# Griffin recurrent block on one core: four edits to the stretch from the gates to the output projection

## The chip, the cores and the metric

One core of a Trainium2 chip runs the whole program. The metric is device time in microseconds (us) of one execution, the median of several runs. Engines are named as in the profile: PE (matrix products), PEld (its weight loads), DVE (vector), ACT (activations), POOL (GpSimd), SP (whose queue issues every DMA here).

## The reference, cut to what matters

Two layers work on 512 tokens of 1024 features in float32: layer 0 is sparse attention and a feed-forward, layer 1 the recurrent block and a feed-forward. The change lies in the recurrent block (1408 channels):

```python
gate, u = jnp.split(h @ w_in, 2, axis=-1)
u = conv(u) + conv_b
r = sigmoid(u @ w_a + b_a); i_g = sigmoid(u @ w_x + b_x)     # in blocks of 88 channels
log_a = -8 * softplus(-lam) * r
a = exp(log_a)
b = sqrt(-expm1(2 * log_a)) * (i_g * u)
_, hs = associative_scan(lin_rec, (a, b), axis=1)            # hs[t] = a[t] * hs[t-1] + b[t]
y = hs * gelu(gate)
return y @ w_out
```

## The kernel before, in words

Activations lie with features on the 128 partitions and the 512 tokens along the row, so 1408 channels are 11 tiles of 128x512. Every float32 product is made of three (lines 259 to 261): weights and activations are split into a high part (`hi`, rounded to the type that PE multiplies) and the rest (`lo`), and hi*hi, hi*lo and lo*hi are summed in a PSUM bank. `chunk` (line 230) loads 1024 columns of weights through SP's queue into one of four `wraw` buffers and splits them in two halves; `split` (line 244) writes `whi` on ACT (line 248) and `wlo` on the engine that the second letter of `how` names (line 254): "av" is DVE, "ag" is POOL. There are six `whi` and six `wlo` buffers of 512 columns, so halves of three chunks.

The instructions are written as loops, and a scheduler orders them. It goes by the instructions' place in the program, shifted by the table `PRIORITY` (line 122: a negative number means that many instructions later than written), and by when its own model has the inputs and a free buffer ready. Each engine then executes its list strictly in order and waits on semaphores. `after` (line 494) adds an order between two instructions.

The recurrent block is `rg` (line 968). `project(t)` (line 973) makes one 128x512 tile of `h @ w_in` from a chunk of weights: 24 products, with the tiles of `gate` being t = 0 to 10. `conv` and `gates` work tile by tile; `gates` leaves r (sigmoid), u (times the input gate, on POOL, line 1031) and vv (a tanh). Then come:
- line 1045, eight of the eleven gate projections, one PSUM bank each;
- lines 1048 to 1053, per tile: Exp on ACT (line 1049), the square of it on POOL into a slot of kind T (line 1052), and (square + 1) times vv on DVE (line 1053);
- lines 1055 to 1059, per tile: Sqrt on ACT (line 1056), the product with u on DVE (line 1058), the scan along the tokens on DVE (line 1059);
- lines 1062 to 1071, per tile: the gate projection (made here for tiles 8 to 10), Gelu from its bank into a slot of kind T (line 1065), the gating product on DVE (line 1067), and the split of y, `yh` on ACT and `yl` on DVE (through lines 248 and 254);
- the output projection `project_out` (line 398): for each of eight tiles of features, two chunks of weights and 33 products over the eleven y, then the residual and the next block.

All Exps stand ahead of all Sqrts on ACT, and these ahead of all Gelus. On-chip memory is given out in slots of 128x512 (line 137): 28 of kind B, 9 of kind T. At the end of the gates u and r hold 11 slots of B each and vv 3; yh and yl take 22 later. The eight PSUM banks are shared by all products.

Of the kernel before, what the change touches and what calls it, by code (L numbers as in the profile page):

```python
# [32 lines left out]
RT = RW // 128  # L33
# [6 lines left out]
def rg_order():  # L40
    """The channels of the recurrent block, tile by tile. Blocks of 88 straddle the tiles of 128; in an even
    tile the part of the block that goes on in the next tile is first, the part of the block from the tile
    before starts in the middle."""
    order, edge = [], []
    for j in range(RT):
        ch = list(range(128 * j, 128 * j + 128))
        p, q = -(128 * j) % BW, (128 * j + 128) % BW
        edge.append((p, q))
        if j % 2 == 0:
            left, full, right = ch[:p], ch[p:128 - q], ch[128 - q:]  # L50
            ch = right + full[:64 - q] + left + full[64 - q:]
        order += ch
    return np.array(order), edge
# [5 lines left out]
def gate_sources(j):  # L59
    """What the gates of tile j need: [(tile, rows of it)] for each product."""  # L60
    if j % 2:
        ends = [(j - 1, 0, RG_EDGE[j - 1][1]), (j + 1, 64, RG_EDGE[j + 1][0])]
        (k, r0, n), short = sorted(ends, key=lambda e: -e[2])
        return [[(j, 0, 128)], [(k, r0, -(-n // 32) * 32), short]]
    return [[(k, 0, 128)] for k in (j - 1, j, j + 1) if 0 <= k < RT]
# [17 lines left out]
def step(name):  # L83
    """All instructions of a method are issued earlier than they are written, as PRIORITY says."""
    def wrap(f):
        def run(self, *a, **k):
            with self.pri(name):
                return f(self, *a, **k)
        return run
    return wrap  # L90


class Split:
    """A weight chunk in two parts that add up to it, by ranges of columns."""
# [12 lines left out]
class Build:  # L107
    def __init__(self, ctx, tc, ins, out):
# [11 lines left out]
    hold = None  # L120
    # how many instructions earlier than written the steps are issued (a digit: in that phase only)
# [4 lines left out]
        "q": -9, "qk": -33, "qr": 20, "res": 140, "scale": 60, "turn": -8, "up": -100, "ws2": -20  # L126
# [18 lines left out]
    def pair(self, dt=F32, name=None):  # L145
        """Two slots in one of the wide ones."""
        t = self.slot("K", dt, name, 1024)
        return t[:, :512], t[:, 512:]

# [12 lines left out]
    def setup(self):  # L162
# [29 lines left out]
        # [diagonal | compressed 0 | diagonal], [diagonal | 0 | compressed 1], compressed 2 and 3  # L192
# [30 lines left out]
    def behind(self):  # L223
        """A piece of the modulations that are needed later."""
        if self.todo:
            l, m, n = self.todo.pop(0)
            with self.pri("ada"):
                self.ada(l, m, n, self.behind_on)
# [15 lines left out]
    def split(self, full, hi, lo, how="av"):  # L244
        """The two parts, on the engines that how names (act, vector, gpsimd)."""
        nc = self.nc
        if how[0] == "a":
            nc.scalar.activation(hi, full, AF.Copy)  # L248
        elif how[0] == "v":
            nc.vector.tensor_copy(hi, full)  # L250
        else:
            nc.gpsimd.tensor_scalar(hi, full, 1.0, 1.0, op0=OP.mult, op1=OP.mult)
        e = nc.vector if how[1] == "v" else nc.gpsimd
        e.tensor_tensor(lo, full, hi.bitcast(F32), op=OP.subtract)  # L254

    def mm3(self, out, w, x, first, last, **k):
        """out += w.T @ x for split operands (hi, lo)."""
        mm = partial(self.nc.tensor.matmul, **k)
        a = mm(out, w[0], x[0], start=first, stop=False)  # L259
        mm(out, w[0], x[1], start=False, stop=False)  # L260
        return a, mm(out, w[1], x[0], start=False, stop=last)  # L261

# [1 line left out]
    def ada(self, l, m, n, engine):  # L264
        """Column n of modulation m of layer l, a partition for each feature of the tile."""
# [15 lines left out]
    def sq_add(self, n, engine, cs=ALL, apart=(KT - 1,)):  # L281
        """Sum of squares over the tiles of features, when a tile (or its columns cs) is final; a new sum
        starts at the tiles in apart."""
# [14 lines left out]
    def norm_scale(self, cs=ALL, behind=None):  # L298
        """1/rms of the tokens cs, the same in all partitions."""
# [6 lines left out]
        for i, t in enumerate(parts):  # L306
            for j in range(nt):
                # all columns share a bank: its first product clears it
                nc.tensor.matmul(p[:, j:j + 1], t[:, 128 * j:128 * j + 128], self.ones[:, 0:1],
                                 start=i == j == 0, stop=t is parts[-1] and j == nt - 1,  # L310
                                 skip_group_check=True)
# [21 lines left out]
    def modulate(self, l, which, cs, R=None):  # L333
        """The input of a block for the tokens cs."""
# [9 lines left out]
    def first(self, src, ts):  # L344
        """Products of the first weight tiles, half of the tokens before the other half."""
# [52 lines left out]
    def project_out(self, src, h, gate, then):  # L398
        """Adds the output to the residual; the last tiles go half of the tokens by half, so that the
        block after it, then, starts with the first half while the second is on its way."""  # L400
# [29 lines left out]
    def nsa(self):  # L430
# [6 lines left out]
        with tc.tile_pool(name="nsa", bufs=1) as np_:  # L437
            self.np_ = np_
            # keys: [window blocks 3..0 | compressed | selected blocks 0..3]
# [54 lines left out]
    def after(self, later, earlier):  # L494
        """Schedule an instruction behind another one, without a wait."""
# [17 lines left out]
    def key_norm(self, banks, r):  # L513
        """Keys of all tokens, normed, every group's twice side by side."""
# [37 lines left out]
    def blocks(self, kv, ct, engine):  # L552
        """Windows of 32 tokens, stride 16: [(parity, d), pair, (group, window)], and the positions."""
# [7 lines left out]
        for gt in range(2):  # L561
            src = ct[gt].rearrange("p (c r) -> p r c", r=16)
            for gp in range(2):
                ph = slice(64 * gp, 64 * gp + 64)
                for jp in range(2):
                    for q in range(4):
                        # token 16 c + 2 jj + jp, jj in 4 q .. 4 q + 3
# [10 lines left out]
    def compress(self, kv, flat):  # L578
        """Hidden layer over the windows, [hidden, (group, window)]."""
        nc = self.nc  # L580
        b = self.bank("tr")
        for c in range(4):
            w = self.raw(self.ins["cmp_w1"][kv, c], 1024)
            for j in range(4):
                for m in range(2):
                    # two groups of sums share a bank: its first product clears both
# [5 lines left out]
        # what the positions add stands behind the windows of group 0  # L592
# [40 lines left out]
    def sel(self, half, tags):  # L633
        """Keys (half 0) or values (1) of the selected branch, with 24 gates each."""
# [15 lines left out]
    def queries(self, g, tags):  # L650
        """Queries of a group for all tokens, two tiles of tokens in a bank."""
        qb = [self.bank(t) for t in tags]
        for k in range(KT):
# [3 lines left out]
            for i in range(NT):  # L657
                s = slice(128 * i, 128 * i + 128)
                # two groups of sums share a bank: its first product clears both
# [24 lines left out]
    def query_tiles(self, g, qn):  # L684
        """Queries with features on the partitions, both parts of a head in one tile."""
        nc = self.nc
        for j, t in enumerate([self.query_norm(*b) for b in qn]):
# [3 lines left out]
            for i in range(2):  # L691
                # even heads: [hi; lo], odd heads: [lo; hi]
# [20 lines left out]
    def attention(self):  # L713
        """Softmaxes run ahead of the products with the values."""
# [48 lines left out]
    def combine(self, g, i, o):  # L763
        """Heads 0, 2 to partitions 0..63 and heads 1, 3 to 64..127 of two tiles."""
# [13 lines left out]
    def softmax(self, g, i, brs, behind):  # L778
        """Probabilities of 4 heads and 128 queries times their gates, by branch and head."""
# [13 lines left out]
        # columns of the scores, and of the mask that goes onto columns of the scores  # L793
# [11 lines left out]
        for h in range(HPG):  # L805
            bank = banks[0][0] if brs == ("c",) and h else self.bank("sc")
            b = bank[:, 32 * h:32 * h + 32] if brs == ("c",) else bank[:, :n]
            # the sums of all heads share the bank of the compressed branch alone: its first product clears it
# [54 lines left out]
    def room(self, i, brs):  # L863
        """How many items' products must be done before slots for these probabilities are free."""
# [12 lines left out]
    def weigh(self, g, i, brs, P, o, first, last):  # L877
        """o += values.T @ P.T, [high parts; low parts of the values] over the partitions."""
# [9 lines left out]
        for u, (n, srcs, V) in enumerate(units):  # L888
# [5 lines left out]
            if n == 32:  # L894
                # both parts below each other, as the values are twice
# [13 lines left out]
    def w_out(self, part):  # L909
        """Adds what the heads of groups 0 and 1 (part 0) or group 2 give to the residual."""  # L910
# [15 lines left out]
    def w_out_last(self, cs):  # L926
        """The same for group 3 and the tokens cs."""
# [13 lines left out]
    def rg_prepare(self):  # L941
        """-8 softplus(-lam), with log1p as a series that keeps float32's accuracy."""
# [25 lines left out]
    def rg(self):  # L968
# [4 lines left out]
        def project(t):  # L973
            if t in early:
                return early[t]
            w = self.chunk(src[t], 1024, "ag" if t < RT else "av")
# [24 lines left out]
        def gates(j):  # L1001
# [5 lines left out]
            for src in ks:  # L1007
# [3 lines left out]
                # the ends of the blocks that straddle, from both neighbours, in one tile  # L1011
# [35 lines left out]
        # tables of the same function together; 1 - a^2 = tanh(x) (1 + a^2) for a = exp(-x)  # L1047
        for j in range(RT):
# [3 lines left out]
            nc.gpsimd.tensor_tensor(t, r[j], r[j], op=OP.mult)  # L1052
            nc.vector.scalar_tensor_tensor(vv[j], t, 1.0, vv[j], op0=OP.add, op1=OP.mult)
        end = e
        for j in range(RT):
            e = nc.scalar.activation(vv[j], vv[j], AF.Sqrt)
            self.after(e.ins, end.ins.name)
            nc.vector.tensor_tensor(vv[j], vv[j], u[j], op=OP.mult)
            nc.vector.tensor_tensor_scan(vv[j], r[j], vv[j], 0.0, op0=OP.mult, op1=OP.add)
        end = e  # L1060
        y = []
        for j in range(RT):
            b = gb[j] if j < 8 else project(j)
            g = self.slot("T")
# [30 lines left out]
def tiles(w):  # L1095
    """[K, N] -> [N/128, 128, K]: for 128 columns, rows k*128+p side by side on partition p."""
# [5 lines left out]
def rows(w, per):  # L1102
    """[K, N] -> [K/128/per, 128, per*N]."""
# [5 lines left out]
def cols(v):  # L1109
    """[..., n*128] -> [128, ...*n]."""  # L1110
# [64 lines left out]
```

## Time and profile before

| what | value |
|---|---|
| median of 3 runs | 1405.46 us (1404.2 to 1409.65) |
| profiled execution: span from its first to its last instruction | 1403.4 us |
| PE busy | 1326.5 us, 95% |
| DVE / ACT / POOL busy | 838.7 / 640.3 / 299.5 us |
| mean granted clock of PE | 0.983 |

Of the profiled execution the span is given; it is 2.1 us below the median and 0.8 us below the lowest of the three runs. A busy share is an average over stages: in each stage another engine can be the one that the others wait for, so what the change touches is read from windows of the trace. A row of the timeline gives the start, the duration, the engine, the line, the output and inputs, how many alike follow each other, and in brackets the idle time of the engine ahead of it with what ended it.

### The profile page before, as it was taken

The numbers are of one execution on the slowest core, as the hardware profiler recorded it, in microseconds if no ns is written. First come the engines' busy times: TensorE is split into PE (matmuls) and PEld (weight loads), VectorE is DVE, ScalarE is ACT, GpSimd is POOL, SyncE is SP. The second block draws the span as 40 slices with busy tenths as digits, with TensorE's granted clock in tenths as the row PEclk, the third lists the DMA queues.
The fourth block names the chain that finished last, engine by engine and source line by source line (L and its number), as shares of the span: only waits on it lengthen the run. The fifth ranks groups of instructions, "written<-read, shape, count | busy, mean of one in ns | idle before, by whom it ended". The sixth has DMA issues, their size and how long they took to land.

```text
span 1403.4 us, 18620 instructions
## 1 busy us (share of the span) xinstructions
PE 1326.5 (95%) x6703; PEld 1095.8 (78%) x6703; DVE 838.7 (60%) x1649; ACT 640.3 (46%) x1446; POOL 299.5 (21%) x367
## 2 busy tenths in 40 slices
PE   6989989889989999999999999977999999999998
PEld 4789956657778888888888977756888888888887
DVE  7885888888987656665532786496354333333231
ACT  4473678857655333333222654834354333332221
POOL 3541254666340000000010032953100000000000
PEclk9999999999999999999999999998999999999999
DMA  7657300222234666665632232212313233333330
GB/s 261 223 186 255 110 1 1 91 73 70 84 91 152 209 206 198 192 197 174 203 100 87 64 106 87 90 51 77 111 63 120 90 102 94 96 96 104 109 107 29
DMA packets 50062, 167.08 MB, mean 119 GB/s; under 512 B 5553, under 2 KB 6833, under 8 KB 49970
## 3 DMA queue, kind: packets, MB, share of 16 engines
q1 hardware_dynamic: 49970, 165.90, 37.6%
q8 instruction: 52, 0.85, 0.2%
q14 instruction: 40, 0.33, 0.1%
HBM read 163.78 MB, written 2.10 MB: 118 GB/s over the span
## 4 chain that ended last, share of the span: by engine, by line
PE 79%; DVE 7%; issue 5%; ACT 5%; POOL 2%; DMA 1%; POOLq 0%; ACTq 0%; SPq 0%; DVEq 0%
PE bank_sc L259 8%; PE bank_sc L260 8%; PE bank_sc L261 8%; PE bank_tr L259 8%; PE bank_tr L260 8%; PE bank_tr L261 8%; PE bank_mm L259 4%; PE bank_mm L260 4%; PE bank_mm L261 4%; PE bank_pv L261 3%; PE bank_pv L259 3%; PE bank_pv L260 3%; PE bank_tr L892 2%; PE bank_sc L811 1%; PE bank_pv L905 1%
## 5 line engine op out<-in xcount | busy, mean ns | idle before, releaser
L248 ACT ACTIVATE whi<-wraw 128x512 fp32r<-128x512 f32 (+4 forms) x422 | 247.9, 595 | 511.5 <-PE bank_tr L260 178.0
L254 DVE TENSOR_TENSOR wlo<-wraw,whi 128x512 fp32r<-128x512 f32 (+2 forms) x368 | 243.5, 667 | 284.4 <-ACT whi L248 283.3
L271 DVE SCALAR_TENSOR_TENSOR wraw<-wraw,cond 128x1024 f32<-128x1024 f32 x96 | 125.6, 1309 | 73.7 <-DMA wraw<-in_ada_w 72.9
L259 PE MATMUL bank_tr<-hh,whi 128*128 128x512 f32 (+1 forms) x400 | 149.8, 375 | 16.4 <-ACT whi L248 10.5
L261 PE MATMUL bank_tr<-hh,wlo 128*128 128x512 f32 (+1 forms) x400 | 149.1, 373 | 6.5 <-POOL wlo L254 6.5
L260 PE MATMUL bank_tr<-hh,whi 128*128 128x512 f32 (+1 forms) x400 | 149.7, 374 | 0.2
L261 PE MATMUL bank_sc<-hh,wlo 128*128 128x512 f32 (+1 forms) x344 | 131.5, 382 | 1.1 <-POOL wlo L254 1.1
L259 PE MATMUL bank_sc<-hh,whi 128*128 128x512 f32 (+1 forms) x344 | 131.5, 382 | 0.0
L260 PE MATMUL bank_sc<-hh,whi 128*128 128x512 f32 (+1 forms) x344 | 131.2, 381 | 0.0
L295 POOL TENSOR_TENSOR sq<-sq 128x256 f32<-128x256 f32 (+1 forms) x25 | 25.7, 1027 | 391.4 <-ACT sq L286 390.8
L254 POOL TENSOR_TENSOR wlo<-wraw,whi 128x512 fp32r<-128x512 f32 (+1 forms) x66 | 94.4, 1446 | 52.7 <-ACT whi L248 47.6
L259 PEld LDWEIGHTS bank_tr<-hh,whi 128*128 128x128 f32 x400 | 76.7, 192 | 31.8 <-ACT whi L248 10.9
L261 PEld LDWEIGHTS bank_tr<-hh,wlo 128*128 128x128 f32 x400 | 76.8, 192 | 20.0 <-POOL wlo L254 7.3
L260 PEld LDWEIGHTS bank_tr<-hh,whi 128*128 128x128 f32 x400 | 77.1, 193 | 13.5 <-DVE hh L254 0.7
L841 POOL TENSOR_SCALAR p<-p,rr 128x128 f32<-128x128 f32 (+3 forms) x128 | 71.5, 577 | 56.5 <-DVE nm L857 27.3
L857 DVE TENSOR_REDUCE nm<-bank_sc 128x1 f32<-128x32 f32 (+4 forms) x192 | 69.7, 382 | 12.6 <-PE bank_sc L816 10.7
L261 PEld LDWEIGHTS bank_sc<-hh,wlo 128*128 128x128 f32 x344 | 65.5, 190 | 13.8 <-POOL wlo L254 1.8
L860 ACT ACTIVATE p<-bank_sc,nm 128x384 f32<-128x384 f32 (+3 forms) x128 | 66.9, 527 | 18.4 <-DVE nm L857 17.7
L260 PEld LDWEIGHTS bank_sc<-hh,whi 128*128 128x128 f32 x344 | 65.6, 191 | 12.2
L259 PEld LDWEIGHTS bank_sc<-hh,whi 128*128 128x128 f32 x344 | 65.5, 190 | 12.2 <-ACT whi L248 0.2
L248 ACT ACTIVATE ph<-bank_tr 128x512 fp32r<-128x512 f32 (+1 forms) x96 | 55.6, 593 | 17.9 <-PE bank_tr L892 16.6
L811 PE MATMUL bank_sc<-K,qs 128*128 128x288 f32 (+5 forms) x128 | 50.3, 396 | 12.4 <-ACT p L860 12.2
(366 smaller groups left out, 3149.7 us busy)
## 6 DMA issues: line engine op xcount, KB each, us to landing
wraw<-in_ada_w SPq DMA_DIRECT2D x96, 512.0 KB, 4.1
wraw<-in_ffn_in SPq DMA_DIRECT2D x88, 512.0 KB, 3.6
wraw<-in_ffn_out SPq DMA_DIRECT2D x32, 512.0 KB, 3.5
wraw<-in_rg_in SPq DMA_DIRECT2D x22, 512.0 KB, 3.2
wraw<-in_ffn_out SPq DMA_DIRECT2D x16, 384.0 KB, 3.2
x<-in_x SPq DMA_DIRECT2D x16, 256.0 KB, 3.5
wraw<-in_nsa_w SPq DMA_DIRECT2D x8, 512.0 KB, 4.3
wraw<-in_cmp_w SPq DMA_DIRECT2D x8, 512.0 KB, 4.4
```

The costliest lines, as they stand in the source:

```text
L248: nc.scalar.activation(hi, full, AF.Copy)
L254: e.tensor_tensor(lo, full, hi.bitcast(F32), op=OP.subtract)
L259: a = mm(out, w[0], x[0], start=first, stop=False)
L260: mm(out, w[0], x[1], start=False, stop=False)
L261: return a, mm(out, w[1], x[0], start=False, stop=last)
L271: done = engine.scalar_tensor_tensor(w, w, 1.0, self.cond, op0=OP.mult, op1=OP.mult, accum_out=mod)
L295: engine.tensor_tensor(s, s, t, op=OP.add)
L811: m = mm(b, q[:, h], kh[:, ks], start=h == 0 or not one, stop=False, skip_group_check=one)
L841: nc.gpsimd.tensor_scalar(P[br, h], P[br, h], r[:, h, x:x + 1], 1.0, op0=OP.mult, op1=OP.mult)
L857: nc.vector.tensor_reduce(nm[:, h, x:x + 1], b[:, cols[br]] if len(brs) > 1 else b, axis=AX, op=OP.max, negate=True)
L860: nc.scalar.activation(dst, b[:, cols[br]] if len(brs) > 1 else b, AF.Exp, bias=nm[:, h, x:x + 1], accum_out=sm[:, h, x:x + 1])
L892: nc.tensor.transpose(t[:n, 128 * h:128 * h + 128], srcs[h], self.ident)
```

## The change

Four edits in `rg`, and one entry in the priority table (edits to comments and blank lines are left out):

```diff
     PRIORITY = {
...
-        "q": -9, "qk": -33, "qr": 20, "res": 140, "scale": 60, "turn": -8, "up": -100, "ws2": -20
+        "q": -9, "qk": -33, "qr": 20, "res": 140, "scale": 60, "scan": -300, "turn": -8, "up": -100, "ws2": -20
     }
...
         def project(t):
             if t in early:
                 return early[t]
-            w = self.chunk(src[t], 1024, "ag" if t < RT else "av")
+            w = self.chunk(src[t], 1024)
...
             t = self.slot("T")
-            nc.gpsimd.tensor_tensor(t, r[j], r[j], op=OP.mult)
+            nc.scalar.activation(t, r[j], AF.Square)
             nc.vector.scalar_tensor_tensor(vv[j], t, 1.0, vv[j], op0=OP.add, op1=OP.mult)
...
             e = nc.scalar.activation(vv[j], vv[j], AF.Sqrt)
             self.after(e.ins, end.ins.name)
-            nc.vector.tensor_tensor(vv[j], vv[j], u[j], op=OP.mult)
-            nc.vector.tensor_tensor_scan(vv[j], r[j], vv[j], 0.0, op0=OP.mult, op1=OP.add)
+            with self.pri("scan"):
+                nc.vector.tensor_tensor(vv[j], vv[j], u[j], op=OP.mult)
+                nc.vector.tensor_tensor_scan(vv[j], r[j], vv[j], 0.0, op0=OP.mult, op1=OP.add)
...
             b = gb[j] if j < 8 else project(j)
-            g = self.slot("T")
+            g = self.slot("B", name="g")
             e = nc.scalar.activation(g, b, AF.Gelu_apprx_tanh)
```

The `wlo` halves of the eleven gate chunks go from POOL to DVE (22 instructions), the eleven squares from POOL to ACT, the eleven Gelu results from kind T to kind B, and the eleven products with u and the scans are ranked 300 instructions later than written. No other line of the program changes, and no DMA is added or taken away.

## Rows read from the trace of the kernel before

**Rows 1.** The page: busy time of each engine over the span.

```profile
PE 1326.5 (95%) x6703; PEld 1095.8 (78%) x6703; DVE 838.7 (60%) x1649; ACT 640.3 (46%) x1446; POOL 299.5 (21%) x367
```

**Rows 2.** Windows: bounds, length, busy us PE, PEld, DVE, ACT, POOL, clock, DMA.

```profile
870.00:893.70 23.70, 20.39 (x84) 14.68 (x83) 9.50 (x10) 11.55 (x21) 16.09 (x16) 1.00 0.24 77
893.70:937.30 43.60, 43.60 (x193) 35.74 (x191) 32.69 (x24) 28.57 (x47) 36.72 (x26) 1.00 0.25 84
937.30:967.80 30.50, 13.51 (x49) 10.47 (x49) 27.08 (x35) 12.07 (x23) 12.77 (x4) 0.72 0.15 48
967.80:1027.00 59.20, 59.20 (x314) 51.09 (x314) 21.36 (x41) 20.12 (x39) 7.18 (x7) 1.00 0.33 97
```

**Rows 3.** What PE waited for from 840 to 1020: us, times, longest.

```profile
PE bank_tr L259 <- ACT whi L248: 10.5, 1, 10.5
PE bank_tr L261 <- POOL wlo L254: 6.5, 1, 6.5
PE bank_sc L259 <- ACT us L248: 1.2, 1, 1.2
PE bank_sc L261 <- POOL wlo L254: 1.1, 1, 1.1
```

**Rows 4.** PE's timeline, 937 to 968 us.

```profile
937.08 0.39 PE L261 MATMUL bank_sc<-hh,wlo 128*128 128x512 f32 x1
947.92 0.79 PE L259 MATMUL bank_tr<-hh,whi 128*128 128x512 f32 x1 [10.45 <-ACT whi L248]
...
955.68 0.80 PE L261 MATMUL bank_tr<-hh,wlo 128*128 128x512 f32 x1 [6.54 <-POOL wlo L254]
...
957.12 0.63 PE L261 MATMUL bank_tr<-hh,wlo 128*128 128x512 f32 x1
...
967.84 0.39 PE L259 MATMUL bank_mm<-yh,whi 128*128 128x512 f32 x1
```

**Rows 5.** ACT's timeline, 907 to 951 us.

```profile
907.09 1.28 ACT L1056 ACT_TABLE_LOAD   x1
...
927.73 0.63 ACT L1065 ACTIVATE slotT<-bank_tr 128x512 f32<-128x512 f32 x1
946.71 0.63 ACT L248 ACTIVATE yh<-slotT 128x512 fp32r<-128x512 f32 x1 [18.35 <-DVE slotT L1067]
947.25 0.61 ACT L248 ACTIVATE whi<-wraw 128x512 fp32r<-128x512 f32 x1
...
949.85 0.57 ACT L1065 ACTIVATE slotT<-bank_sc 128x512 f32<-128x512 f32 x1
```

**Rows 6.** DVE's timeline, 869 to 949 us.

```profile
869.86 0.74 DVE L994 SCALAR_TENSOR_TENSOR u<-slotT,vec,u 128x509 f32<-128x509 f32 x1
...
921.71 1.78 DVE L1058 TENSOR_TENSOR vv<-vv,u 128x512 f32<-128x512 f32 x1
...
932.28 1.26 DVE L1058 TENSOR_TENSOR vv<-vv,u 128x512 f32<-128x512 f32 x2
...
935.72 1.26 DVE L1058 TENSOR_TENSOR vv<-vv,u 128x512 f32<-128x512 f32 x2
...
946.02 1.86 DVE L1067 TENSOR_TENSOR slotT<-slotT,vv 128x512 f32<-128x512 f32 x3
```

**Rows 7.** One line at a time: ns min/median/max, first and last start (L254: 860 to 975).

```profile
L1053 DVE SCALAR_TENSOR_TENSOR vv<-slotT,vv x11: 1511/1526/1786, 901.8 to 920.0; 128x512 f32<-128x512 f32 x11
L254 POOL TENSOR_TENSOR wlo<-wraw,whi x22: 1282/1724/7682, 879.2 to 959.0; 128x512 fp32r<-128x512 f32 x22
L254 DVE TENSOR_TENSOR wlo<-wraw,whi x16: 285/558/1780, 859.7 to 973.7; 128x512 fp32r<-128x512 f32 x6, 128x256 fp32r<-128x256 f32 x6, 128x384 fp32r<-128x384 f32 x2, 128x128 fp32r<-128x128 f32 x2
L254 DVE TENSOR_TENSOR yl<-slotT,yh x11: 678/681/1002, 947.8 to 970.5; 128x512 fp32r<-128x512 f32 x11
```

**Rows 8.** ACT's timeline, 380 to 412 us: Exp, then Square.

```profile
381.91 0.23 ACT L860 ACTIVATION_READ_ACCUMULATOR p<-bank_sc,nm 128x1 f32 x1
...
390.70 0.42 ACT L286 ACTIVATE sq<-x 128x256 f32<-128x256 f32 x1 [1.26 <-DVE x L368]
```

## The prediction

> **What bounds the kernel now.** I read the page first, then windows over the recurrent block, then what PE waited for, then the timelines of PE, ACT and DVE around the longest wait. PE is busy 95% of the span [rows 1], so only PE's idle or slow time can be won, and only where the change acts. The windows show where that is. In 893.7:937.3 PE is busy without a gap; in 937.3:967.8 it is busy 13.51 of 30.50 us, at a granted clock of 0.72; in 967.8:1027 it is full again, 59.20 of 59.20 us, with DMA busy for a third of the time [rows 2]. So what follows would not absorb a gain: an earlier start of the output projection is an earlier end.
>
> The hole is two waits, 10.5 us for a `whi` from ACT and 6.5 us for a `wlo` from POOL [rows 3]. PE starts its last product before them at 937.08, the next gate projection at 947.92, stops again until 955.68, and reaches the first product of the output projection at 967.84 [rows 4]. After the idle time its products take 0.63 us instead of 0.39 for a while [rows 4]: the lower of the clock's two levels, 1.2 GHz instead of 2.4.
>
> Why ACT is late: after its sixth Gelu at 927.73 it stands for 18.35 us at the first `yh`, which needs the first gating product from DVE; the `whi` that PE wants is the next in ACT's list [rows 5]. Why DVE is late: it has gone through all line-1053 operations (the last at 920.0) and all eleven pairs of product and scan before the first gating product at 946.02 [rows 6, 7]. And these run slowly: line 1053 takes a median of 1526 ns beside POOL's squares and splits [rows 7], against 0.74 us for the same operation in the convolution; two pairs take 3.44 us (932.28 to 935.72) once POOL is quiet, while the first product alone took 1.78 us beside POOL [rows 6]. POOL suffers as well: its `wlo` takes 1282 ns at best and 7682 at worst, the one that PE stands for until 955.68 [rows 4, 7]. So the stage hangs on DVE and POOL slowing each other, and on one instruction in the wrong place of ACT's list.
>
> **The change, part by part.**
>
> *Splits to DVE.* 22 halves leave POOL and cost DVE 0.68 us each, the median of `yl`, the same operation on the same shape [rows 7]; back to back I count 0.61, the step of three gating products in 1.86 us [rows 6]. PE's 6.5 us wait for POOL has no cause left. The halves made before 897 share DVE with the last convolution tile, whose chain PE also waits for (1.2 us), while 1.1 us of waiting for a POOL `wlo` goes [rows 3]. Bounds for that stage: three splits in the convolution's way at the slowest DVE split of the trace, 1.78 us [rows 7], 5.3 us lost; or all of PE's 3.3 us of idle time (23.70 - 20.39) gained [rows 2]. I take 1.0 gained, near the wait that is named, since the convolution waits for other engines too and leaves DVE room (busy 9.50 of 23.70 us [rows 2]).
>
> A DVE split beside POOL work has taken up to 1.78 us where 0.68 is usual [rows 7]. The Trainium skill, "SBUF — State Buffer", section "SBUF: two separate sides", says that a DVE operation with two SBUF inputs and a GpSimd one exclude each other for the whole of the instruction. By that rule each of the three splits would wait out one POOL operation, 3 x (0.68 + 1.28) = 5.9 us lost instead of 1.0 gained, and the sum below would be 12.2 instead of 19.1. The slow rows agree with it; how often the two meet before 897 no row tells.
>
> *Squares to ACT.* The Exps and a few splits end at 907.09 [rows 5]. A Square of half the length takes 0.42 us [rows 8], a copy of the full length 0.63 [rows 5]: eleven add 4.6 to 6.9 us, I take 6.4, near the full length. The Sqrt table (1.28 us [rows 5]) is loaded at about 913.5 and the first Sqrt done at about 915.5. Before, the first product with u started at 921.71, behind line 1053 [rows 6]; at 0.74 us each line 1053 takes DVE 8 us and keeps up with the squares. So ACT's added work is paid by the time that its Sqrts no longer wait for DVE.
>
> *Gelu results in B.* The sixth Gelu runs at 927.73, the seventh at 949.85 [rows 5]: T has nine slots and they are given back late. B has three free when the Gelus begin, and each finished pair gives back two (u and r). With pairs from 915.5 seven are done by 927.7, 17 slots for eight Gelus. Cost nothing, hidden by PE's projections; if the pairs were late, ACT would wait at a Gelu instead.
>
> *Scans ranked later.* Nothing is removed. Wherever a split, a gating product or a `yl` is ready it goes ahead of the next pair, so the first y come out before the last scans, and ACT's first `yh` waits for one or two pairs at most. No DMA moves and SP's list keeps its order; POOL's loses 33 instructions and nothing is put behind a wait there.
>
> *The sum on PE.* After 937.30 two projections of 24 products at 0.226 us (43.60 us for 193 [rows 2]) are left: 10.9 us, so the output projection could start at 948.2, not 967.84 [rows 4]. That is 19.6 us: 17.0 of waits and 2.6 of slow clock and restart.
>
> *Can y keep up?* This is the next limit. DVE from 915.5: eleven pairs at 1.72 = 18.9; gating and `yl`, 22 x 0.61 = 13.4; the eight halves of gate tiles 7 to 10, 4.9; four pieces of the first output weights, 1.9. Together 39.1, so y10 is ready at 954.6 if DVE never idles. PE wants y10 at 948.2 plus 30 products = 955.0. It is a tie. Bounds: no loss, or, if DVE starts the pairs only at 921.71 as before, 921.71 + 39.1 - 955.0 = 5.8 us and a slow restart like the old one, 7 in all. I take 1.5 lost, near the lower end, as the cause of the old start, POOL's squares, is gone.
>
> Total: 19.6 + 1.0 - 1.5 = 19.1 us less. The profiled span would go from 1403.4 to 1384.3. It stands 2.1 us below the median of the runs, which I leave as it is: 1405.46 - 19.1 = **1386.4 us**. Bounds of the terms: 19.6 + 3.3 = 22.9 at best (1382.6), 19.6 - 5.3 - 7 = 7.3 at worst (1398.2).
>
> **The rivals.**
>
> *DVE becomes the bound* (chance 0.20, part of "faster"): the pairs start late or DVE idles between gating and `yl`, and PE stops in the first output tile. With 5.8 to 7 us lost there the gain is 13 to 15 us, about 1392. For it: the tie, and DVE's 27.08 of 30.50 us in the old hole [rows 2]. Against: what fills that window is work that POOL had pushed back.
>
> *Scans behind splits that wait for PE* (chance 0.07 for no change, 0.04 for slower). A `wlo` of the output weights may only overwrite a buffer that PE has finished with. If the new rank puts such splits ahead of the scans in DVE's list, the scans wait for PE and PE then for y. With six buffers, the last piece for the first output tile waits for the end of the projection before the last, 942.8; then 18.9 + 13.4 us bring y10 to 975.1, where the old kernel wanted it at 967.84 + 6.8 = 974.6: no change, 1406. Behind the splits for the second output tile, which wait until 948.2, y10 comes at 980.5, 6 us after the old time: with a slow restart about 1413. It decides from the point where the first scan stands behind the last piece for the first output tile. Against it: the scheduler issues what is ready, and while such a split waits a scan is ready.
>
> *A table load at each switch between Exp and Square* (chance 0.01, slower). If Square were not in the table set that Exp needs, up to 22 loads of 1.28 us [rows 5] would put 28 us on ACT ahead of the Sqrts: pairs from 943.5, y10 at 982.6, 8 us after the old time, about 1414. The rows speak against it: at 390.70 a Square follows the Exp whose sum is read at 381.91, and no load stands between [rows 8]. The Trainium skill, "ScalarE: Activation LUTs", section "Table sets: the hidden batching unit", asks for calls batched by set and names copy, relu, identity and abs as members of every set, not Square; this trace shows the pair without a load.
>
> *The hole stays* (chance 0.04, no change): ACT's list again has a `yh` ahead of the `whi` that PE needs, with DVE far behind. For the full 17 us DVE's first gating product would have to be near 946 again; with pairs from 915.5 and three splits even all eleven pairs first end by 936.3, and PE would lose nothing much. For the old time some further delay of 10 us on DVE is needed, and no row shows one without POOL.
>
> **How the numbers follow.** Half a per cent, 7.0 us, is about what a measurement of this kernel can tell from no change. My forecast's own case has 0.64, with 1382 to 1390; with DVE as the bound (0.20) faster has 0.84. No change has 0.07 + 0.04 = 0.11, slower 0.04 + 0.01 = 0.05. The range from 1381 to 1398 takes in both faster cases and the worst sum of the terms; what lies above it is most of the last 0.16.
>
> **What would show it.** Right: PE without the two waits and at a clock of 1.00 from 893 to 975; the first product on `yh` near 948; POOL idle from 897 on; line 1053 near 0.74 us; gating products between pairs on DVE; no ACT_TABLE_LOAD at the squares' line. Wrong: PE waiting for a `yh` or `yl` in the first output tile for over 6 us; ACT idle for over 10 us at a Gelu or a `yh`; DVE idle while a pair's inputs are ready; a `wlo` on DVE over 1.5 us between 870 and 897 with PE waiting for the convolution; or a change of PE's waits outside 870 to 975, where I expect none.

## The result, and the profile after

The changed kernel takes 1385.61 us, the median of five runs (1384.67 to 1394.47), against 1405.46 before: a ratio of 0.9869, with a 95% interval of 0.984 to 0.9899. Measured once more beside another set of runs of before (median 1407.67), it was 1385.66 us and 0.9836 (0.9806 to 0.9867). The prediction was 1386.4, in a range of 1381 to 1398.

The profiled execution is the longest of the five: 1392.5 us between its first and last instruction. Almost 11 us of that were lost long before the changed code, in the attention part: the edge product, the first product on the gates' last edge tile of 48 rows, starts at 888.09 us instead of 877.17, though every engine's list is the same up to that time. So the two traces are compared from that product on, and the windows below are those of [rows 2], moved by 10.92 us. First the page's busy line of after [rows 1], then the windows (bounds, length, busy us of PE, PEld, DVE, ACT, POOL, clock, DMA).

```profile
PE 1329.4 (95%) x6703; PEld 1097.6 (79%) x6703; DVE 830.6 (60%) x1671; ACT 644.6 (46%) x1457; POOL 245.2 (18%) x334
```

```profile
880.92:904.62 23.70, 21.39 (x89) 15.77 (x88) 10.93 (x15) 12.17 (x23) 10.10 (x11) 1.00 0.26 89
904.62:948.22 43.60, 43.60 (x194) 36.11 (x193) 35.39 (x52) 37.03 (x65) 1.29 (x1) 1.00 0.28 90
948.22:978.72 30.50, 29.39 (x126) 23.26 (x125) 23.30 (x39) 15.04 (x30) 1.29 (x1) 1.00 0.28 83
978.72:1037.92 59.20, 57.47 (x356) 50.97 (x355) 28.35 (x64) 25.97 (x57) 8.53 (x8) 1.00 0.31 97
```

The third row is the old hole: PE is busy 29.39 us of 30.50 where it was 13.51, at a clock of 1.00 where it was 0.72, and POOL does 1.29 us where it did 12.77. PE's 1.7 idle us in the last row lie at the start of the next block, which before came behind the end of the row. Of what PE still waits for in the stretch, three lines, against [rows 3]:

```profile
PE bank_sc L261 <- DVE wlo L254: 1.6, 1, 1.6
...
PE bank_mm L259 <- ACT yh L248: 0.5, 1, 0.5
...
PE bank_mm L260 <- DVE yl L254: 0.5, 2, 0.2
```

Both long waits are gone. The 1.6 us are a gate half on DVE, in the early stage; the other two stand in the first output tile. PE's timeline shows the places, and the landmarks used from here on: the edge product, the first product on `yh`, and the first product of the second output tile (`bank_sc<-yh`), which comes when all eleven y have been used once (in one run, u_scan, after ten; see there).

```profile
888.09 0.49 PE L259 MATMUL bank_tr<-edge,whi 48*128 48x512 f32 x1 [0.46 <-POOL edge L1016]
...
896.84 0.50 PE L261 MATMUL bank_sc<-hh,wlo 128*128 128x512 f32 x1 [1.60 <-DVE wlo L254]
...
957.77 0.39 PE L259 MATMUL bank_mm<-yh,whi 128*128 128x512 f32 x1
...
966.18 0.50 PE L259 MATMUL bank_mm<-yh,whi 128*128 128x512 f32 x1 [0.53 <-ACT yh L248]
966.90 0.50 PE L260 MATMUL bank_mm<-yl,whi 128*128 128x512 f32 x1 [0.22 <-DVE yl L254]
...
967.47 0.39 PE L259 MATMUL bank_sc<-yh,whi 128*128 128x512 f32 x1
```

From the edge product, the first `yh` product comes after 957.77 - 888.09 = 69.68 us; before it was 967.84 - 877.17 = 90.67 [rows 4]. The second tile comes after 79.38 us; before, it was 975.32 - 877.17 = 98.15. The two rows of before:

```profile
877.17 0.49 PE L259 MATMUL bank_tr<-edge,whi 48*128 48x512 f32 x1 [0.46 <-POOL edge L1016]
...
975.32 0.39 PE L259 MATMUL bank_sc<-yh,whi 128*128 128x512 f32 x1
```

I call this last length **the stage**. It is 18.8 us shorter.

Why, on DVE, by its timeline (compare [rows 6]):

```profile
910.51 0.69 DVE L1053 SCALAR_TENSOR_TENSOR vv<-slotT,vv 128x512 f32<-128x512 f32 x1
...
926.32 0.69 DVE L1059 TENSOR_TENSOR vv<-vv,u 128x512 f32<-128x512 f32 x1 [1.09 <-ACT vv L1056]
...
936.72 0.68 DVE L1068 TENSOR_TENSOR g<-g,vv 128x512 f32<-128x512 f32 x1
937.32 1.28 DVE L254 TENSOR_TENSOR wlo<-wraw,whi 128x512 fp32r<-128x512 f32 x2
...
961.41 0.67 DVE L254 TENSOR_TENSOR wlo<-wraw,whi 128x512 fp32r<-128x512 f32 x1
...
963.39 0.68 DVE L254 TENSOR_TENSOR wlo<-wraw,whi 128x512 fp32r<-128x512 f32 x1
...
966.16 0.69 DVE L254 TENSOR_TENSOR yl<-g,yh 128x512 fp32r<-128x512 f32 x1 [0.70 <-ACT yh L248]
```

Line 1053 takes 0.69 us where its median was 1.53 [rows 7]. The first product with u comes 38.23 us after the edge product instead of 44.54, and the first gating product after seven products and five scans, not after all eleven pairs. Directly behind it stand two halves of a gate tile's weights. Between 926.32 and the 0.70 us ahead of the last `yl` the timeline marks no idle time of DVE.

And on ACT: the squares (line 1052), the load for the Sqrts, and the Gelus (compare [rows 5]).

```profile
923.21 1.13 ACT L1052 ACTIVATE slotT<-r 128x512 f32<-128x512 f32 x2
924.36 1.28 ACT L1056 ACT_TABLE_LOAD   x1
925.65 0.63 ACT L1056 ACTIVATE vv<-vv 128x512 f32<-128x512 f32 x1
...
937.43 0.63 ACT L248 ACTIVATE yh<-g 128x512 fp32r<-128x512 f32 x1 [2.48 <-DVE g L1068]
937.97 0.61 ACT L248 ACTIVATE whi<-wraw 128x512 fp32r<-128x512 f32 x1
938.49 0.58 ACT L1066 ACTIVATE g<-bank_tr 128x512 f32<-128x512 f32 x1
```

No load stands between Exp and Square. The first `yh` costs ACT 2.48 us of waiting, not 18.35. And the Gelus no longer run ahead six at a time: from the second on, each comes between two `yh`.

### The profile page after: what moved, and what is told of

The parts are those of the page before. It is cut to its first block, busy times and chain, and to the rows that moved or that the text cites. A ratio compares the mean times of both kernels' runs of the same rounds, so it can differ in the third digit from the quotient of the medians.

```text
span 1392.5 us, 18615 instructions
## 1 busy us (share of the span) xinstructions
PE 1329.4 (95%) x6703; PEld 1097.6 (79%) x6703; DVE 830.6 (60%) x1671; ACT 644.6 (46%) x1457; POOL 245.2 (18%) x334
## 4 chain that ended last, share of the span: by engine, by line
PE 78%; DVE 10%; issue 5%; ACT 5%; DMA 2%; POOL 1%; POOLq 0%; ACTq 0%; SPq 0%; DVEq 0%
PE bank_sc L259 8%; PE bank_sc L260 8%; PE bank_sc L261 8%; PE bank_tr L260 8%; PE bank_tr L259 8%; PE bank_tr L261 8%; PE bank_mm L260 3%; PE bank_mm L259 3%; PE bank_mm L261 3%; PE bank_pv L261 3%; PE bank_pv L259 3%; PE bank_pv L260 3%; PE bank_tr L892 2%; DVE wraw L271 2%; PE bank_sc L811 2%
## 5 line engine op out<-in xcount | busy, mean ns | idle before, releaser
L254 DVE TENSOR_TENSOR wlo<-wraw,whi 128x512 fp32r<-128x512 f32 (+3 forms) x390 | 256.0, 663 | 282.7 <-ACT whi L248 277.4
L841 POOL TENSOR_SCALAR p<-p,rr 128x128 f32<-128x128 f32 (+3 forms) x128 | 71.6, 580 | 56.3 <-DVE rr L832 19.3
L857 DVE TENSOR_REDUCE nm<-bank_sc 128x1 f32<-128x32 f32 (+4 forms) x192 | 69.7, 381 | 16.8 <-PE bank_sc L816 14.2
L860 ACT ACTIVATE p<-bank_sc,nm 128x384 f32<-128x384 f32 (+3 forms) x128 | 66.9, 527 | 18.8 <-DVE nm L857 17.9
L260 PEld LDWEIGHTS bank_sc<-hh,whi 128*128 128x128 f32 x344 | 64.7, 188 | 12.2
L254 POOL TENSOR_TENSOR wlo<-wraw,whi 128x512 fp32r<-128x512 f32 (+1 forms) x44 | 53.5, 1231 | 31.8 <-ACT whi L248 30.8
```

Source lines behind the costliest of these rows:

```text
L841: nc.gpsimd.tensor_scalar(P[br, h], P[br, h], r[:, h, x:x + 1], 1.0, op0=OP.mult, op1=OP.mult)
L857: nc.vector.tensor_reduce(nm[:, h, x:x + 1], b[:, cols[br]] if len(brs) > 1 else b, axis=AX, op=OP.max, negate=True)
L860: nc.scalar.activation(dst, b[:, cols[br]] if len(brs) > 1 else b, AF.Exp, bias=nm[:, h, x:x + 1], accum_out=sm[:, h, x:x + 1])
```

## The experiments

The kernels are compared by the stage, since the whole time varies by some 10 us between executions of one kernel, mostly in the attention part. "First u" is the first product with u on DVE, "first y" the first product on `yh`, both in us after the edge product; "rest" is what is left from the end of the stage to the last instruction. These four come from one profiled execution each. Every ratio is to runs of before beside it on the same chip, whose medians were 1405.46 to 1407.67. The lines of later kernels are shifted by a few.

| kernel | first u | first y | stage | rest | median us (ratio to before, 95%) |
|---|---|---|---|---|---|
| before | 44.5 | 90.7 | 98.15 | 428.0 | 1405.46 |
| after | 38.2 | 69.7 | 79.38 | 425.0 | 1385.61 (0.984 to 0.9899) |
| after_again | 38.3 | 69.7 | 79.46 | 425.0 | 1385.66 (0.9806 to 0.9867) |
| u_split | 39.1 | 71.2 | 86.86 | 428.8 | 1393.64 (0.9901 to 0.9944) |
| u_square | 39.7 | 71.6 | 83.03 | 427.5 | 1393.75 (0.9886 to 0.995) |
| u_scan | 38.2 | 77.7 | 84.53 | 426.3 | 1392.97 (0.987 to 0.9933) |
| u_slot | 38.3 | 74.6 | 82.04 | 425.1 | 1390.46 (0.9862 to 0.9918) |
| o_pool | 38.2 | 84.1 | 91.58 | 427.9 | 1400.73 (0.9933 to 0.9972) |
| u_pool | 44.5 | 85.9 | 94.92 | 427.8 | 1402.65 (0.9946 to 0.9982) |
| v_half | 35.1 | 69.7 | 77.87 | 425.0 | 1384.56 (0.9814 to 0.9872) |
| v_half_again | 35.2 | 69.7 | 77.91 | 427.8 | 1383.25 (0.9799 to 0.9866) |
| v_sqd | 37.5 | 69.7 | 78.94 | 425.1 | 1383.31 (0.9803 to 0.988) |
| v_g2 | 38.2 | 69.7 | 79.03 | 427.5 | 1386.36 (0.9813 to 0.9892) |
| v_halfg2 | 35.1 | 69.7 | 77.17 | 428.3 | 1382.11 (0.9792 to 0.9857) |

**How far to trust the stage.** The changed kernel once more.

> The kernel after once more, unchanged: how far does the length of the stage vary between profiled executions? If it is set by the instructions' own times, 79.2 to 79.6 us again (79.38 in the first profile), whatever the span. If it varies like the span does, by several us, none of the differences below 3 us between the kernels is worth anything.

79.46 against 79.38, with spans of 1385.4 and 1392.5. The second kernel run twice, v_half, gave 77.87 and 77.91. So, as far as two kernels profiled twice can show, differences of a few tenths of a us can be read from the stage, which the medians can't give.

**One edit undone at a time.** u_split gives the low halves of the gate weights back to POOL.

```diff
-            w = self.chunk(src[t], 1024)
+            w = self.chunk(src[t], 1024, "ag" if t < RT else "av")
```

> The change with one edit undone: the low halves of the gate weights back on POOL. 'Stage' is the time from the first product on the 48-row edge tile to the first product of the second output tile; it is 98.2 us in the profile before and 79.4 after, 18.8 of the 21.8 us between the two profiles from that point to the end. Theory A (DVE and POOL slow each other, and a POOL half can take 7.7 us beside a busy DVE): from the first pair on DVE is never idle, so POOL's halves for tiles 8 to 10 take 1.8 to 3.2 us each as before, and PE waits for one of them again; stage 82 to 90 us. Theory B (only the place of instructions in the lists counts; who makes the halves does not): DVE has 13 us less to do, y comes sooner, stage 77 to 79 us.

The stage is 86.86, 7.5 us longer, in the range of theory A (POOL and DVE slow each other); a stage under 79.38 would have said that DVE is better off without the halves, and it did not come. But the path is not the one that A expected: in the last projections PE waits for no half from POOL. It stops at the y, as its waits (first line), a product and two windows show:

```profile
PE bank_mm L259 <- ACT yh L248: 2.3, 4, 0.9
```

```profile
957.86 0.63 PE L261 MATMUL bank_mm<-yh,wlo 128*128 128x512 f32 x1
```

```profile
955.00:960.00 5.00, 3.72 (x8) 1.55 (x8) 4.41 (x9) 3.71 (x8) 0.00 (x0) 0.78 0.14 39
960.00:965.00 5.00, 4.36 (x11) 2.66 (x11) 3.85 (x8) 2.92 (x6) 0.00 (x0) 0.53 0.47 144
```

DVE's scans, products and splits beside POOL take 1.8 to 2.2 us where they take 0.7 to 1.2 alone (the scan of line 1060 has a mean of 1395 ns against 1207 in after). One such scan, and the POOL instruction beside it:

```profile
916.08 2.21 DVE L1060 TENSOR_TENSOR_SCAN vv<-r,vv 128x512 f32<-128x512 f32 x1
```

```profile
915.92 1.29 POOL L254 TENSOR_TENSOR wlo<-wraw,whi 128x512 fp32r<-128x512 f32 x1 [1.70 <-ACT whi L248]
```

So the y come late one by one, PE waits a little at the last ones, and after these waits the clock falls to 0.53 in the second window, near the lower level: the last seven products of the tile take 0.63 to 0.80 us.

u_square gives the squares back to POOL.

```diff
-            nc.scalar.activation(t, r[j], AF.Square)
+            nc.gpsimd.tensor_tensor(t, r[j], r[j], op=OP.mult)
```

> The change with one edit undone: the squares back on POOL. Theory A: eleven squares alone keep POOL busy for 14 to 16 us, line 1053 takes about 1.5 us again beside them, but squares on ACT end at about the same time (the last at 924.3 us in the profile after), so the first pair starts within 2 us of where it does now; stage 78 to 82 us, no difference that the timing can tell. Rival: any work of POOL beside DVE costs PE time; line 1053 would end 5 us or more later and the stage be 84 us or more.

83.03: 3.7 us longer, between what A and the rival gave. Line 1053 has a mean of 1293 ns against 684, so the slowing is there. But the first product with u is only 1.5 us later, since ACT, freed of 6.3 us of squares (eleven of 616 ns), reaches its Sqrts earlier. PE then stops for 1.4 us at a low half from DVE and 1.7 us at a `yh`. That edit moved work as much as it removed a collision.

u_scan takes the rank of product and scan away, u_slot puts the Gelu results back into kind T.

```diff
-        "q": -9, "qk": -33, "qr": 20, "res": 140, "scale": 60, "scan": -300, "turn": -8, "up": -100, "ws2": -20
+        "q": -9, "qk": -33, "qr": 20, "res": 140, "scale": 60, "turn": -8, "up": -100, "ws2": -20
```

> The change with one edit undone: product and scan ranked where they are written. In DVE's list all eleven pairs then stand ahead of the two halves for the gate projection of tile 8. Theory C (the place of the gate halves in DVE's list decides): the pairs start where they do now and end 19.5 us later, the second of these halves is ready about 21 us after the first product, 6 us after PE wants it; PE waits 5 to 7 us for a low half from DVE, and loses 1 to 2 more at the lower clock: stage 85 to 88 us. Theory A alone (POOL was the whole cause): the order on DVE is of no weight, stage 79 to 81 us.

```diff
-            g = self.slot("B", name="g")
+            g = self.slot("T")
```

> The change with one edit undone: the Gelu results back in slots of kind T. The lists then have three Gelus ahead of the first yh, four yh ahead of the next two high halves on ACT, and on DVE five gating products and five yl ahead of the halves for tile 8. Theory C: PE waits about 4 us for the halves of tile 8, and the last y comes 2 to 3 us later than in the change: stage 82 to 85 us. Theory A alone, or the reading of the prediction (the kind of slot costs nothing): stage 79 to 80 us.

u_scan: 84.53, 5.2 us longer; u_slot: 82.04, 2.7 longer. u_slot is in the range of C (the place of instructions in the lists decides), u_scan just short of it. But u_scan's landmark flatters it: there PE starts the second tile ahead of the last y of the first.

```profile
963.86 0.39 PE L259 MATMUL bank_sc<-yh,whi 128*128 128x512 f32 x1
964.53 0.50 PE L259 MATMUL bank_mm<-yh,whi 128*128 128x512 f32 x1 [0.28 <-ACT yh L248]
...
965.59 0.39 PE L261 MATMUL bank_mm<-yh,wlo 128*128 128x512 f32 x1
965.82 0.40 PE L259 MATMUL bank_sc<-yh,whi 128*128 128x512 f32 x1
```

At 965.82 the first tile is done, and three products of the second with it, so like for like the stage is 965.82 - 3 x 0.227 - 879.32 = 85.8 us: 6.4 longer than in after, and within C's range. In u_scan POOL is silent and the first product with u as early as in after. DVE then does all eleven pairs without a pause, and the `wlo` that PE needs comes after them and a gating product; DVE's list, then PE's stop:

```profile
934.83 2.33 DVE L1060 TENSOR_TENSOR_SCAN vv<-r,vv 128x512 f32<-128x512 f32 x2
937.08 0.67 DVE L1068 TENSOR_TENSOR g<-g,vv 128x512 f32<-128x512 f32 x1
937.66 1.29 DVE L254 TENSOR_TENSOR wlo<-wraw,whi 128x512 fp32r<-128x512 f32 x2
```

```profile
938.40 0.80 PE L261 MATMUL bank_sc<-hh,wlo 128*128 128x512 f32 x1 [5.09 <-DVE wlo L254]
```

In u_slot several Gelus run ahead, their `yh` follow, and the gate halves come behind those: PE waits 0.5 us and 0.8 us for a `whi` and 1.0 for a `wlo` (2.3 together, where C had about 4), and its first `yh` product is 4.9 us later than in after. All eleven y are then ready in time (82.04 - 74.56 = 7.48 us for the tile, as before), so 2.2 of the 4.9 come back.

**Two edits together.** o_pool is the kernel before with the work taken off POOL alone, by the diff below; u_pool is its mirror image, after with the same lines put back.

```diff
-            w = self.chunk(src[t], 1024, "ag" if t < RT else "av")
+            w = self.chunk(src[t], 1024)
...
-            nc.gpsimd.tensor_tensor(t, r[j], r[j], op=OP.mult)
+            nc.scalar.activation(t, r[j], AF.Square)
```

> The kernel before with the gate weights' low halves on DVE and the squares on ScalarE, and neither the scan's rank nor the Gelu results in B. The stage is the time from the 48-row edge product to the first product of the second output tile: 98.15 us before, 79.38 after. Theory A (DVE and POOL slow each other, and their work beside each other is most of the 18.8 us): L1053 near 0.69 us, the first product with u about 38 us after the edge product, and 84 to 89 us for the stage, the rest being one stop of PE at a low half that stands behind seven gating products and their yl in DVE's list. Theory C (the order of the lists is most of it): 93 us or more, with PE again waiting over 10 us near the last gate projections. Median by A 1393 to 1397, by C 1401 or more.

> The kernel after with both kinds of POOL work given back (low halves of the gate weights and squares on POOL), the scan's rank and the Gelu results in B kept: the mirror image of the run above. Alone, the two edits cost the stage 7.5 and 3.7 us. Theory A: they add up or more, since the one's POOL time delays the other's: 89 to 95 us, L1053 on DVE 1.3 us or more in the mean, the slow DVE operations at about 1.5 to 1.8 us. Theory C: the order alone holds most of the gain: 85 us or less. Median by A 1397 to 1402, by C 1393 or less.

o_pool: 91.58, which neither theory gave; nor is the median, 1400.73, in the range of either. Relieving POOL alone is worth 98.15 - 91.58 = 6.6 us. Line 1053 is fast (685 ns) and the first product with u as early as in after, as A has it, but PE stops for 12.0 us at one low half:

```profile
950.04 0.80 PE L261 MATMUL bank_sc<-hh,wlo 128*128 128x512 f32 x1 [12.01 <-DVE wlo L254]
```

On DVE that half stands behind eleven pairs, eight gating products and six `yl`, the last of them at 948.70. It is the old hole with DVE in POOL's place.

u_pool: 94.92, at the upper end of A's range; the median, 1402.65, is just above it. Placing alone is worth 98.15 - 94.92 = 3.2 us. Here it is the old hole with the old culprit, the `yh` ahead of the `whi` in ACT's list; first ACT, then PE, then line 1053:

```profile
937.84 0.63 ACT L248 ACTIVATE yh<-g 128x512 fp32r<-128x512 f32 x1 [14.59 <-DVE g L1068]
938.38 0.58 ACT L1066 ACTIVATE g<-bank_tr 128x512 f32<-128x512 f32 x1
938.85 0.62 ACT L248 ACTIVATE whi<-wraw 128x512 fp32r<-128x512 f32 x1
```

```profile
939.52 0.80 PE L259 MATMUL bank_sc<-hh,whi 128*128 128x512 f32 x1 [6.95 <-ACT whi L248]
```

```profile
L1053 DVE SCALAR_TENSOR_TENSOR vv<-slotT,vv 128x512 f32<-128x512 f32 x11 | 17.2, 1614 | 15.4 <-POOL slotT L1052 15.4
```

So of 18.8 us, 6.6 come from POOL's relief alone, 3.2 from the placing alone, and the other 9.0 only from both: a fast DVE that does its work in the wrong order still leaves PE waiting, and a good order on a slow DVE does too. That the four single edits, undone, sum to 7.5 + 3.7 + 6.4 + 2.7 = 20.3, near the 18.8, is chance; by pairs the same sum is 15.5 + 12.2 = 27.7.

**What the last 2.2 us hang on.** In after the first output tile takes 79.38 - 69.69 = 9.7 us instead of 7.48. v_half gives every second square to DVE, which is partly idle while ACT does Exps and squares.

```diff
-            nc.scalar.activation(t, r[j], AF.Square)
+            if j % 2:
+                nc.vector.tensor_tensor(t, r[j], r[j], op=OP.mult)
+            else:
+                nc.scalar.activation(t, r[j], AF.Square)
```

> The kernel after with every second square moved from ScalarE to DVE, where DVE waits for ScalarE anyway. Theory D (from the first Sqrt on DVE is never idle, and PE's 2.2 us of waiting for y in the first output tile are set by the time of that first Sqrt): the Sqrt comes 2.5 to 3.5 us earlier (first product with u 35 to 36 us after the edge product instead of 38.2), the wait for yh and yl goes, and the stage takes 77.0 to 78.0 us instead of 79.38. Rival E (the two halves of the second output tile that stand ahead of the ninth and tenth yl on DVE set it, or y follows PE's projections): the stage stays at 79.0 to 79.8. Median by D 1383 to 1385, by E as after.

> The kernel with every second square on DVE once more, beside the kernel after on the same chip. Theory D: stage 77.7 to 78.1 us again (77.87 in its first profile), 1.3 to 1.7 below after; median 0.5 to 2.5 us below after. Rival (chance): stage as after, 79.2 or more.

77.87 and 77.91, as D had it. The first product with u is 3.1 us earlier and DVE waits only 0.33 us ahead of it, and the two halves of the second output tile still stand ahead of a `yl`, now the tenth and the eleventh. 1.5 of the 2.2 us are gone; three of the last four `yl` still wait for their `yh`, for 0.37 to 0.70 us.

v_sqd puts all squares on DVE.

```diff
-            nc.scalar.activation(t, r[j], AF.Square)
+            nc.vector.tensor_tensor(t, r[j], r[j], op=OP.mult)
```

> The kernel after with all squares on DVE and none on ScalarE. Theory D (DVE's work from the first line 1053 on is what y waits for): six more squares of 0.6 us on DVE than with every second one there are 3.7 us, and DVE had only 1.9 us of idle time left, so y comes later again: stage 78.5 to 81. Rival (ScalarE's time up to the Sqrts is what counts, DVE has room): the first Sqrt comes still earlier and the stage goes to 77.2 or less.

78.94: D again. DVE has no marked idle time from 900 us, in the midst of the squares, to the last `yl`, its first product with u is back at 37.5, and PE waits 1.0 us for a `yh`. Of the three ways to share the squares, half on each engine is the best by the stage; the medians on the same chip (1383.25 and 1383.31) don't tell the last two apart.

v_g2 gives the Gelu results two slots of their own, v_halfg2 joins that to v_half.

```diff
-    SLOTS = {"A": 24, "B": 28, "K": 8, "T": 9}
+    SLOTS = {"A": 24, "B": 28, "K": 8, "T": 7, "G": 2}
...
-            g = self.slot("B", name="g")
+            g = self.slot("G", name="g")
```

> The kernel after with the Gelu results in two slots of their own (T 7, B 28), so that two Gelus instead of one run ahead. Theory F (slots of a kind are handed out in the order of the program, so in B a Gelu comes only after the yl of the tile before, and that puts the gate halves ahead of most y on ScalarE and DVE): with two ahead some gate halves come later and y earlier, the stage lies between 79.4 and 82.0 (82.03 with the results in T, where three to six bunch), the first output product comes later than 69.7 us after the edge product, and the output tile waits less for y. Rival (the kind of slot does not matter, the loss of u_slot is chance): first output product within 0.5 of 69.7 and stage within 0.5 of 79.4.

> Every second square on DVE, and the Gelu results in two slots of their own (T 7). If the two small gains in the stage, 1.5 and 0.35 us, come from different places, they add up: 77.3 to 77.7. If the second is chance or hangs on the same wait for y: 77.8 to 78.3. PE's bare work in the stage is 77.1 us (79.38 less 2.2 us of waiting for y), so below 77.1 by neither.

v_g2: 79.03 with the first `yh` product at 69.70, which are the rival's numbers: what theory F gave for the time did not come. In ACT's list the Gelus do run two ahead, so F's account of the order stands, but one more Gelu ahead costs nothing; u_slot, with three ahead of the first `yh`, lost 2.7 us, and no run lies between. v_halfg2: 77.17, a little under the 77.3 to 77.7 that the sum of the two gains would give, so neither stands in the other's way. PE waits for no y in the stage, and its first output tile takes 7.48 us again. By the stage it beats after by 2.2 to 2.3 us; the medians, 1382.11 and 1385.66 us on the same chip, agree but have intervals that overlap.

## Why the prediction was right, point by point

*The sum.* From the edge product to the last product on an edge of 72 rows, with which the early stage ends (891.14 before, 900.81 after), 13.97 us became 12.72: 1.25 gained, where 1.0 was taken. From there to the first `yh` product, 76.70 became 56.96: 19.7 gained, where 19.6 was worked out. The first output tile grew from 7.48 to 9.70: 2.2 lost, where 1.5 was taken. Together 18.8, where 19.1 was predicted. The medians fell by 19.9 us and, beside the second set of runs, by 22.0. That 1386.4 lies within 1 us of both medians of after is in part luck, since the median of before moved by 2.2 us from one set to the next.

*Splits to DVE: right in kind, wrong in place.* In the early stage POOL's wait and ACT's (1.14 and 1.25 us) were replaced by one of 1.6 on DVE, within the bounds. The slowest half on DVE there took 1.09 us, beside POOL's edge copies. The Trainium skill, "SBUF — State Buffer", section "SBUF: two separate sides", lets a two-input DVE operation and a GpSimd one exclude each other; the 5.9 us that this could have cost by the prediction's estimate did not come, while u_pool's line 1053, 1614 ns against 684, agrees with it. That "PE's 6.5 us wait for POOL has no cause left" holds, but the halves undone cost 7.5 us mostly through late y, a path that the prediction did not price.

*Squares to ACT: right.* 6.4 us were taken, 6.3 measured. The first Sqrt was to be done at 915.5 in the time of before; it was done at 926.28 - 10.92 = 915.4. The table-load rival fell: no load between Exp and Square.

*Gelu results in B: the effect was missed.* The step said "cost nothing", as B has room, and gave the edit no part in the sum; undone, it is worth 2.7 us. Room was not the point. By my reading, slots of a kind are given out in the order of the program: in B a tile's Gelu result, `yh` and `yl` follow each other, so the scheduler places a Gelu only behind the `yl` of the tile before, which keeps `yh` from running ahead of the gate halves on ACT. v_g2 fits this, as two slots let two run ahead. That u_slot lost by the order its trace shows: four `yh` stand ahead of a `whi` that PE waits for. That the order of slots made that order is argued, not shown. That T's nine slots, given back late, stopped ACT behind the sixth Gelu does not hold once POOL is silent: in o_pool seven run in a row.

*Scans ranked later: right, and worth more than was said.* They let the first y out before the last scans. But of the hole the prediction said that with all eleven pairs first "PE would lose nothing much". The pairs did end in time, at 937.16 in u_scan, which is 935.0 in the time of before against the 936.3 worked out; but PE wanted the `wlo` behind them 5.1 us before it got it. u_scan lost 6.4 us that way, and o_pool 12.0 in one stop.

*The tie for y: near, by two terms short.* y10 was worked out for 954.6 and wanted at 955.0. In the time of before the last `yl` ended at 966.85 - 10.92 = 955.9, and PE wanted it at 957.77 - 10.92 + 30 x 0.227 = 953.7; that is the 2.2 us lost. DVE being the next limit was right, as v_half and v_sqd show from both sides, and as a rival with 5.8 to 7 us of loss it came to 2.2. One term left out is the halves of the second output tile, 2 x 0.6 us, that the list has ahead of the ninth and tenth `yl`. The other is that what PE gains in the early stage makes it want the y sooner: the 1.0 gained and the 1.5 lost were added as if they did not touch each other.

*Elsewhere.* From the end of the stage on after was 3.0 us shorter in its first profile (428.0 to 425.0). That need not be the change: v_half and its repetition are the same kernel and have 425.0 and 427.8. The difference goes with the granted clock some 60 us behind the stage. In the profiles where it stays at 1.00 there, the rest is 425.0 to 425.1 (u_scan like for like); where it falls, as in before, 427.5 to 428.8. Whether the change makes the fall rarer, two profiles of after and one of before can't tell. Here are the windows of v_half, then of v_half_again:

```profile
1019.00:1034.00 15.00, 14.56 (x120) 14.24 (x120) 10.46 (x28) 11.53 (x28) 0.82 (x1) 1.00 0.25 72
```

```profile
1013.00:1028.00 15.00, 14.57 (x99) 14.25 (x100) 8.59 (x24) 8.79 (x23) 0.82 (x1) 0.82 0.22 70
```

## What to carry to other kernels

When one engine stops for another, look at what stands ahead of the needed instruction in that engine's list: here relief of POOL and DVE and a better order were worth 6.6 and 3.2 us alone, and 18.8 together. The buffer pool that a result lives in can change the order of the lists: here the kind of slot alone was worth 2.7 us, and the count of free slots did not foretell it. Where the whole time scatters by more than the effect, measure between two landmarks on the engine that sets the end; it repeated to 0.1 us where spans differed by 7. Check in each run that the landmark still means the same work: in u_scan it did not, by 1.3 us.

## What the runs showed of the hardware that was not expected

The short waits at the y cost more than their sum. In after PE's listed waits in the first output tile come to 1.0 us (0.53, 0.23 and 0.22), and the tile took 2.2 us longer than 7.48, at a clock of 1.00 throughout. Products start 0.23 us apart but are listed at 0.39 us each, or 0.50 behind a stop, so the listed idle time is less than the loss. In u_split the listed waits come to 3.4 us (2.3, 0.7 and 0.4), and the tile took 86.86 - 71.22 = 15.6 us instead of 7.48. Of these 8.2 us, 4.5 were lost before the first product of 0.63 us, at 957.86: 10.4 us for 26 products that take 5.9 without a stop. And the same program, v_half, once kept the clock at 1.00 and once fell to 0.82 in the same 15 us, behind 15 us in which PE was busy 13.71 us the one time and 13.83 the other.
